# Rotated queries and keys of the second layer through SBUF with their low parts on GpSimd, and the norm after the out projection done in PSUM

## The chip, the core and the metric

The program runs on one core of one Trainium2 chip. The metric is the device time of one execution in microseconds (us). TensorE (PE, with its weight loads PEld), VectorE (DVE), ScalarE (ACT) and GpSimd (POOL) work side by side, each through its own instructions in the order in which the program has them; nearly all DMAs are issued by SyncE (SP), in order too. An instruction that waits therefore holds up all that stands behind it on its engine.

## The reference, cut to what matters

One inference step of a trunk of two layers over a prompt of 1024 tokens and 8 single sample tokens that attend to 2048 cached ones. Layer 0 has forgetting attention (12 heads of 64), layer 1 differential attention with rotary positions (6 heads of 2 x 64). Both have four more heads on a memory, one joint out projection, and a SwiGLU.

```python
# layer 1
q = rope(z[..., :w].reshape(b, t, 2 * N_HEADS_DIFF, HEAD_DIM), pos)
k = rope(z[..., w:2 * w].reshape(b, t, 2 * N_HEADS_DIFF, HEAD_DIM), pos)
s1 = einsum('bqhd,bkhd->bhqk', qb[..., :HEAD_DIM], k[..., :HEAD_DIM]) * HEAD_DIM ** -0.5   # s2 likewise
weights = masked_softmax(s1, mask) - lam * masked_softmax(s2, mask)
...
# both layers
h = h + rms_norm(merged @ w_out, g_post_mix)
u = rms_norm(h, g_pre_ffn) @ w_gate_up
```

## The kernel before

All is fp32. A matmul operand is split into a high part (a copy that TensorE's fast fp32 form rounds, `hi`, on ACT) and a low part (source minus high part, `lo`), and a projection is three products: high x high, high x low, low x high. The prompt's tokens, with the samples at their end, lie in three thirds of 384, 384 and 264 columns.

In `mixer` a loop goes over six pairs of heads, `hp`. While the attention of pair `hp` runs (`parts`, as steps that `beat` places between matmuls), `project` makes the queries (a = 0), keys (1) and values (2) of pair `hp + 1`, each for three thirds: nine blocks of 24 matmuls (`mm3`). A block adds up in one bank of PSUM with the tag "g". There are two such banks, so a block cannot begin until the last reader of the block two before it is done. In layer 1 a block of queries or keys goes on like this:

- `rope`: DVE shuffles neighbouring rows out of the bank into `sw` in SBUF (L998), POOL multiplies `sw` by the sine table (L999), DVE multiplies the bank by the cosine table in place (L1001) and adds `sw` to it in place (L1002).
- queries, `q_split`: ACT scales each half (64 rows) by 0.125 from the bank into `qq` (L403), SP copies it to the other half's place (L404), DVE makes the low part `ql` from the bank (L406).
- keys, `k_split`: ACT copies the bank to `f` (L1175), from which the outputs are transposed later (`natural`), then makes the high parts `kk` (L170); DVE makes the low parts (L173, `kk<-g,kk`).

Then come the scores `s_d` (two matmuls a piece, with `qq` and `ql`), `peaks` on DVE (L447: adds the causal rows, negates and takes the peak), the exponential on ACT (L463), the merge of the two weightings on DVE (`p_d`, L552), transposes `tp_d`, and the product with the values `av_d`. ACT moves that into `ao_d` (L1191), DVE norms it later (L1199), SP stores it (L1201). The memory heads have `ao_m` with the same tag "ao" (L519, L520).

Alongside runs `decode`: SP loads a page of cached keys `kp` (L602), POOL multiplies it by the query (L616), DVE adds up (L620), and the buffer is free for another page.

After the mixer, `finish_tile` with a name that begins with "o" handles a tile of 128 tokens after the out projection (8 tiles and the samples in each layer, in the groups FA, FB, FC of three): TensorE transposes the tile into `y_o`, two banks with the tag "s2" of which there is one set; ACT squares and adds up (L338), ACT copies `y_o` to `yn_o` in SBUF (L170); DVE and POOL make the root (L329, L333); DVE multiplies (L387) and adds to `h_o` (L388). A second norm of the sum (L338, L345) gives what TensorE transposes back (`xt_o`) for the FFN.

TensorE's order is pinned to the order in which the program was written; for the other engines a list scheduler sets it when the program is built.

Of the kernel before, what the change touches and what calls it, by code (L numbers as in the profile page):

```python
# [9 lines left out]
F32 = mybir.dt.float32  # L10
# [3 lines left out]
ALU = mybir.AluOpType  # L14
# [81 lines left out]
class Step:  # L96
# [274 lines left out]
    def finish_tile(self, pool, acc, o, ti, hsrc, hdst, g_post, g_pre, x, name, wait, row=None):  # L371

        nc = self.nc
        r = self.rows(ti)
        h = self.load_h(pool, ti, hsrc, f"h_{name}")
        y = pool.tile([128, D], F32, name=f"yn_{name}", tag="nat")
        if row is None:
            yp = self.b2(f"y_{name}")
            for k in range(8):
                self.pe.transpose(yp[:r, k * 128 : (k + 1) * 128], acc(k)[:, o : o + r], self.ident)  # L380
            ss = self.sumsq(pool, yp[:r], r, y, f"sy_{name}")
            self.hi(y[:r], yp[:r])
            row = y
        else:
            ss = self.sumsq(pool, row[:r], r, y, f"sy_{name}")
        rs = self.rstd(pool, ss[:r], r, D, f"ry_{name}")
        nc.vector.scalar_tensor_tensor(y[:r], row[:r], rs[:r], g_post[:r], op0=ALU.mult, op1=ALU.mult)  # L387
        nc.vector.tensor_tensor(h[:r], h[:r], y[:r], op=ALU.add)  # L388
        nc.sync.dma_start(hdst(ti), h[:r])
        if x is not None:  # L390
            self.norm(pool, h, r, g_pre, y, name)
            yield wait
            self.to_x(y, r, lambda tv, k0: [(tv, x[:, k0 : k0 + 4])], o, name)


    def q_split(self, src, n, c0, qq, ql):


        nc = self.nc
        part = lambda a, e, c: a[64 * e : 64 * e + 64, c : c + n]  # L400
        for e in range(2):
            same = part(qq[e], e, c0)
            nc.scalar.activation(same, part(src, e, 0), AF.Copy, scale=0.125)  # L403
            nc.sync.dma_start(part(qq[e], 1 - e, c0).bitcast(F32), same.bitcast(F32))  # L404
        for e in range(2):
            nc.vector.scalar_tensor_tensor(  # L406
                part(ql[e], e, c0), part(src, e, 0), 0.125, part(qq[e], e, c0).bitcast(F32),
                op0=ALU.mult, op1=ALU.subtract,
            )

    def k_split(self, src, n, c0, kk):
# [4 lines left out]
        for e in range(2):  # L416
            self.lo(part(kk[e], 1 - e, c0), part(src, e, 0), part(kk[e], e, c0))
# [22 lines left out]
    def peaks(self, pool, s, last, bias, name):  # L440
# [3 lines left out]
        if last is not None:  # L444
# [3 lines left out]
            out=s, in0=s, in1=bias, scale=-1.0, scalar=3e38, op0=ALU.add, op1=ALU.min, accum_out=nm  # L448
# [77 lines left out]
    def self_part(self, pool, qq, ql, kk, vs, subs, qb, bias, width, done, name):  # L526
# [9 lines left out]
        def make(i, e):  # L536
            b = bias(e, w)
            s, last = self.scores(qq[e], ql[e], kk[e], qb, w, f"s_{name}{e}")
            nm = self.peaks(pool, s, last if merge is None else None, b, f"{name}{e}")
# [453 lines left out]
    def rope(self, pool, ps, n, t, st, name):  # L993

        nc = self.nc
        sw = pool.tile([128, 384], F32, name=f"rs_{name}", tag="rsw")
# [5 lines left out]
        nc.vector.tensor_tensor(ps[:, :n], ps[:, :n], sw[:, :n], op=ALU.add)  # L1002
# [38 lines left out]
    def mixer(self, l, xs, st, begin):  # L1041
# [5 lines left out]
        with ExitStack() as cx:  # L1047
# [3 lines left out]
            if l == 1:  # L1051
# [3 lines left out]
                {**bufs, **{f"ql{i}{e}": 1 for i in range(2) for e in range(2)}, "kvf": 6 - 3 * l, "pt": 3 - l, "ao": 7 - 2 * l, "at": 1, "sm": 16, "st": 8},  # L1055
# [95 lines left out]
            def project(hp, r, units=(0, 1, 2), thirds=(0, 1, 2)):  # L1151
                for a in units:
# [8 lines left out]
                    for t in thirds:  # L1161
# [7 lines left out]
                        if a < 2 and l == 1:  # L1169
                            self.rope(main, ps, n, t, st, nm)  # L1170
                        if a == 0:
                            self.q_split(ps, n, t0 * 128, r["qq"], r["ql"])
                        else:
                            f = main.tile([128, 384], F32, name=f"f{nm}", tag="kvf")
                            nc.scalar.activation(f[:, :n], ps[:, :n], AF.Copy)  # L1175
                            if a == 1:
                                self.k_split(ps, ks(t), t0 * 128, r["kk"])
                            self.spawn(natural(a, t, hp, f, r), RD if a == 1 and l == 1 else 4.0)
# [531 lines left out]
```

## Time and profile before

| | us |
|---|---|
| median of 3 runs | 3060.92 |
| lowest and highest | 3060.40, 3066.18 |
| the profiled execution | 3070.34 |
| its span, first to last instruction | 3068.5 |
| PE busy in the span | 2806.3 |
| DVE, ACT, POOL busy | 2068.0, 1767.4, 1107.1 |

The profile is of one execution, whose own time is 9.4 us above the median. Busy times of different engines overlap. For TensorE the profile also gives the granted clock, as a share of 2.4 GHz; its two levels here are 1.00 and 0.50. Layer 1's mixer stands at 1557 to about 2140 us of the span; its six projections of queries, keys and values end at about 2006 us. The norms after the out projection stand at 630 to 735 (layer 0) and 2155 to 2260 us (layer 1), and the short third of each near 1300 and 2810 us.

### The profile page before, as it was taken

To read this page: it belongs to the slowest core of one execution; us is meant where nothing else is said; L and a number is where in the kernel's file an instruction comes from. 1 tells how busy PE (TensorE), PEld (TensorE's weight loads), DVE (VectorE), ACT (ScalarE), POOL (GpSimd) and SP (SyncE) were. 2 spreads that over 40 slices of the span, in tenths; PEclk is the share of its full clock that TensorE was granted. 3 is DMA by queue.
4 is the path that set the end of the run, shared out by engine and by line. 5 is a ranking of instruction groups with operands and counts; after the bars stand their busy time and mean duration, and the time that the engine had idled before them with its cause. 6 is when DMAs were issued, how large, how long until landed. Compare 5 with 4: busy or idle time off the path is not lost. (4 is left out here: it accounts for less than half of the span.)

```text
span 3068.5 us, 53791 instructions
## 1 busy us (share of the span) xinstructions
PE 2806.3 (91%) x17567; PEld 2647.2 (86%) x17567; DVE 2068.0 (67%) x3645; ACT 1767.4 (58%) x4617; POOL 1107.1 (36%) x840
## 2 busy tenths in 40 slices
PE   7999998878999999999988888888888999999998
PEld 5899998877888998999977878888877899899998
DVE  7566666577678777386466778755887667654655
ACT  6445555444678886355554554465543689864544
POOL 3345556422211111244434556564232111113443
PEclk9999999989999999999999999899998999999999
DMA  5555566486556654356645444464775566644764
GB/s 167 154 154 162 161 170 184 115 263 201 165 184 198 200 191 160 109 164 196 185 148 154 125 124 123 125 179 144 249 229 172 176 226 220 204 148 128 226 180 132
DMA packets 523979, 529.01 MB, mean 172 GB/s; under 512 B 54957, under 2 KB 416078, under 8 KB 523698
## 3 DMA queue, kind: packets, MB, share of 16 engines
q1 hardware_dynamic: 523554, 524.79, 56.2%
q8 instruction: 138, 2.26, 0.3%
q14 instruction: 143, 1.17, 0.1%
q0 software_dynamic: 144, 0.79, 0.1%
HBM read 477.82 MB, written 39.24 MB: 169 GB/s over the span
## 5 line engine op out<-in xcount | busy, mean ns | idle before, releaser
L700 ACT ACTIVATE vp<-vp,s 128x64 f32<-128x64 f32 (+1 forms) x1680 | 462.5, 358 | 119.0 <-DMA vp<-in_cache_fox_v_dram 67.7
L81 PE MATMUL ga<-xf,h_g 128*128 128x384 f32 (+1 forms) x2112 | 499.3, 324 | 0.0
L81 PE MATMUL gu<-xf,h_u 128*128 128x384 f32 (+1 forms) x2112 | 495.1, 321 | 0.0
L81 PE MATMUL g<-xi,h_w 128*128 128x384 f32 (+2 forms) x1728 | 438.7, 340 | 49.7 <-DVE kk L173 23.8
L616 POOL TENSOR_TENSOR kp<-kp,qb 128x768 f32<-128x768 f32 x186 | 344.1, 1852 | 324.5 <-DMA kp<-in_cache_fox_k_dram 140.8
L81 PE MATMUL dn<-h_d,gt 128*128 128x512 f32 x1056 | 352.9, 408 | 20.1 <-ACT gt L170 16.4
L81 PEld LDWEIGHTS ga<-xf,h_g 128*128 128x128 f32 x2112 | 368.2, 191 | 2.0 <-ACT fa L1434 0.2
L81 PEld LDWEIGHTS gu<-xf,h_u 128*128 128x128 f32 x2112 | 365.0, 189 | 0.2
L81 PEld LDWEIGHTS g<-xi,h_w 128*128 128x128 f32 x1728 | 304.5, 197 | 60.8 <-DVE ql L406 26.0
L81 PE MATMUL ga<-xf,l_g 128*128 128x384 f32 (+1 forms) x1056 | 339.4, 321 | 0.0
L81 PE MATMUL gu<-xf,l_u 128*128 128x384 f32 (+1 forms) x1056 | 338.6, 321 | 0.8 <-POOL l_u L173 0.8
L173 POOL TENSOR_TENSOR l_u<-r_u,h_u 128x512 fp32r<-128x512 f32 x96 | 135.1, 1407 | 496.1 <-ACT h_u L170 489.3
L708 DVE TENSOR_TENSOR acc<-acc,vp 128x768 f32<-128x768 f32 x240 | 248.9, 1043 | 77.3 <-ACT vp L700 75.9
L81 PE MATMUL g<-xi,l_w 128*128 128x384 f32 (+2 forms) x864 | 284.9, 330 | 3.8 <-DVE rs_x L329 1.9
L173 POOL TENSOR_TENSOR l_d<-r_d,h_d 128x512 fp32r<-128x512 f32 x96 | 136.1, 1418 | 401.9 <-ACT h_d L170 370.0
L1436 DVE TENSOR_TENSOR fa<-fa,dn 128x512 f32<-128x512 f32 (+1 forms) x400 | 227.5, 578 | 65.3 <-PE dn L81 64.2
L81 PEld LDWEIGHTS dn<-h_d,gt 128*128 128x128 f32 x1056 | 203.7, 194 | 75.9 <-ACT gt L170 20.5
L81 PE MATMUL dn<-l_d,gt 128*128 128x512 f32 x528 | 214.2, 406 | 9.1 <-DVE l_d L173 8.2
L173 POOL TENSOR_TENSOR l_g<-r_g,h_g 128x512 fp32r<-128x512 f32 x96 | 140.6, 1465 | 200.2 <-ACT h_g L170 197.9
L170 ACT ACTIVATE h_u<-r_u 128x512 fp32r<-128x512 f32 x192 | 120.0, 628 | 149.0 <-PE dn L81 59.2
L81 PEld LDWEIGHTS ga<-xf,l_g 128*128 128x128 f32 x1056 | 200.8, 190 | 0.0
L81 PEld LDWEIGHTS gu<-xf,l_u 128*128 128x128 f32 x1056 | 199.1, 189 | 1.1 <-POOL l_u L173 1.0
(590 smaller groups left out, 6305.8 us busy)
## 6 DMA issues: line engine op xcount, KB each, us to landing
kp<-in_cache_fox_k_dram SPq DMA_DIRECT2D x128, 384.0 KB
r_g<-in_w_gate_up_dram SPq DMA_DIRECT2D x192, 256.0 KB
r_u<-in_w_gate_up_dram SPq DMA_DIRECT2D x192, 256.0 KB
r_d<-in_w_down_dram SPq DMA_DIRECT2D x192, 256.0 KB
vp<-in_cache_fox_v_dram SPq DMA_DIRECT2D x128, 384.0 KB
kp<-in_cache_diff_k_dram SPq DMA_DIRECT2D x128, 384.0 KB
vp<-in_cache_diff_v_dram SPq DMA_DIRECT2D x128, 384.0 KB
r_wo<-in_w_out_dram SPq DMA_DIRECT2D x96, 256.0 KB
```

What stands on the lines that cost most here:

```text
L81: self.pin(self.eng.matmul(out, w, x, **k), max(n, 256) if x.dtype == F32R else 2 * max(2 * n, 256))
L170: self.nc.scalar.activation(out, src, AF.Copy)
L173: (eng or self.nc.vector).tensor_tensor(out, src, hi.bitcast(F32), op=ALU.subtract)
L616: r = eng.tensor_tensor(k, k, q, op=ALU.mult)
L700: nc.scalar.activation(dst[:, hs], v[:, hs], AF.Copy, scale=wv[:, b, h, g : g + 1])
L708: todo.append(nc.vector.tensor_tensor(acc[b], acc[b], v, op=ALU.add))
L1436: self.last_v = nc.vector.tensor_tensor(dst, dst, o, op=ALU.add).ins.name
```

## The change

It has three parts.

1. In layer 1 `rope`'s last addition writes a new tile `f` in SBUF (tag "kvf") instead of the bank; `q_split` and `k_split` read `f`, so that the addition is the bank's last reader. ACT's copy of the keys to `f` goes. The low parts are made by POOL. The queries are no longer scaled by 0.125; `peaks` applies the factor to the scores.
2. The buffers of layer 1's mixer: "kvf" has 4 instead of 3, "ao" 3 instead of 5.
3. In `finish_tile`, where the name begins with "o", ACT's copy of `y_o` goes; DVE multiplies in place in PSUM and adds from there, so that the addition is the last reader of `y_o`.

```diff
@@ finish_tile
-        y = pool.tile([128, D], F32, name=f"yn_{name}", tag="nat")
+        y = at = pool.tile([128, D], F32, name=f"yn_{name}", tag="nat")
...
-            self.hi(y[:r], yp[:r])
-            row = y
+            if name[0] == "o":
+
+                row = at = yp
+            else:
+                self.hi(y[:r], yp[:r])
+                row = y
...
-        nc.vector.scalar_tensor_tensor(y[:r], row[:r], rs[:r], g_post[:r], op0=ALU.mult, op1=ALU.mult)
-        nc.vector.tensor_tensor(h[:r], h[:r], y[:r], op=ALU.add)
+        nc.vector.scalar_tensor_tensor(at[:r], row[:r], rs[:r], g_post[:r], op0=ALU.mult, op1=ALU.mult)
+        nc.vector.tensor_tensor(h[:r], h[:r], at[:r], op=ALU.add)
@@ q_split (its scale is a new argument, 0.125 by default), k_split (eng, None by default)
-            nc.scalar.activation(same, part(src, e, 0), AF.Copy, scale=0.125)
+            nc.scalar.activation(same, part(src, e, 0), AF.Copy, scale=scale)
...
+            if scale == 1.0:
+                self.lo(part(ql[e], e, c0), part(src, e, 0), part(qq[e], e, c0), nc.gpsimd)
+                continue
...
-            self.lo(part(kk[e], 1 - e, c0), part(src, e, 0), part(kk[e], e, c0))
+            self.lo(part(kk[e], 1 - e, c0), part(src, e, 0), part(kk[e], e, c0), eng)
@@ peaks (scale is 0.125 where the two weightings are merged, layer 1)
-            out=s, in0=s, in1=bias, scale=-1.0, scalar=3e38, op0=ALU.add, op1=ALU.min, accum_out=nm
+            out=s, in0=s, in1=bias, scale=-scale, scalar=3e38, op0=ALU.add, op1=ALU.min, accum_out=nm
@@ rope
+        f = pool.tile([128, 384], F32, name=f"rf_{name}", tag="kvf")
...
-        nc.vector.tensor_tensor(ps[:, :n], ps[:, :n], sw[:, :n], op=ALU.add)
+        nc.vector.tensor_tensor(f[:, :n], ps[:, :n], sw[:, :n], op=ALU.add)
+        return f
@@ mixer
-"kvf": 6 - 3 * l, "pt": 3 - l, "ao": 7 - 2 * l,
+"kvf": 6 - 2 * l, "pt": 3 - l, "ao": 7 - 4 * l,
@@ project
                         if a < 2 and l == 1:
-                            self.rope(main, ps, n, t, st, nm)
-                        if a == 0:
+                            f = self.rope(main, ps, n, t, st, nm)
+                            if a == 0:
+                                self.q_split(f, n, t0 * 128, r["qq"], r["ql"], 1.0)
+                            else:
+                                self.k_split(f, ks(t), t0 * 128, r["kk"], nc.gpsimd)
+                        elif a == 0:
```

TensorE's own order does not change. On POOL, where the queries of the fourth pair of heads are made, the program before has these rows (`rs<-rs,tab` is the sine multiplication of a third, 384, 384 and 256 wide; `kp` a page; `l_w` a low part of weights):

```order
L999 TENSOR_TENSOR rs_23314<-rs_23314,tab_20410 128x384
L616 TENSOR_TENSOR kp_10_1_23389<-kp_10_1_23389,qb_1_22668 128x768
L616 TENSOR_TENSOR kp_11_1_23465<-kp_11_1_23465,qb_1_22668 128x768
L999 TENSOR_TENSOR rs_23433<-rs_23433,tab_20411 128x384
L616 TENSOR_TENSOR kp_12_1_23557<-kp_12_1_23557,qb_1_22668 128x768
L173 TENSOR_TENSOR l_w_23548<-r_w_23544,h_w_23546 128x8x2x32
L173 TENSOR_TENSOR l_w_23872<-r_w_23868,h_w_23870 128x512
L999 TENSOR_TENSOR rs_23518<-rs_23518,tab_20411 128x256
```

and the changed one, at the same place:

```order
L1010 TENSOR_TENSOR rs_23306<-rs_23306,tab_20402 128x384
L626 TENSOR_TENSOR kp_10_1_23381<-kp_10_1_23381,qb_1_22662 128x768
L173 TENSOR_TENSOR ql_20376<-rf_23305,qq_23230 64x384
L173 TENSOR_TENSOR ql_20377<-rf_23305,qq_23231 64x384
L626 TENSOR_TENSOR kp_11_1_23458<-kp_11_1_23458,qb_1_22662 128x768
L1010 TENSOR_TENSOR rs_23426<-rs_23426,tab_20402 128x384
L626 TENSOR_TENSOR kp_12_1_23551<-kp_12_1_23551,qb_1_22662 128x768
L173 TENSOR_TENSOR l_w_23542<-r_w_23538,h_w_23540 128x8x2x32
L173 TENSOR_TENSOR ql_20376<-rf_23425,qq_23230 64x384
L173 TENSOR_TENSOR ql_20377<-rf_23425,qq_23231 64x384
L173 TENSOR_TENSOR l_w_23863<-r_w_23859,h_w_23861 128x512
L1010 TENSOR_TENSOR rs_23512<-rs_23512,tab_20402 128x256
```

Two low parts of a third now stand ahead of the next third's sine multiplication.

On DVE, from the second third's addition to the third third's cosine, before:

```order
L1002 TENSOR_TENSOR g_23344<-g_23344,rs_23433 128x384
L447 ISA s_d_23498,nm_d_23501<-s_d_23498,zm 128x384
L447 ISA nm_d_23501 128x1
L620 TENSOR_REDUCE s_20345<-kp_11_1_23465 128x12
L552 SCALAR_TENSOR_TENSOR p_d_23401<-p_d_23449,f_d_23477,p_d_23401 128x256
L998 STREAM_SHUFFLE rs_23518<-g_23458 128x256
L1001 TENSOR_TENSOR g_23458<-g_23458,tab_20410 128x256
L406 SCALAR_TENSOR_TENSOR ql_20385<-g_23344,qq_23239 64x384
L406 SCALAR_TENSOR_TENSOR ql_20386<-g_23344,qq_23240 64x384
```

and in the change:

```order
L1013 TENSOR_TENSOR rf_23425<-g_23336,rs_23426 128x384
L561 TENSOR_SCALAR f_d_23470<-r_d_23221,l_d_23220,le 128x1
L454 ISA s_d_23491,nm_d_23494<-s_d_23491,zm 128x384
L454 ISA nm_d_23494 128x1
L630 TENSOR_REDUCE s_20336<-kp_11_1_23458 128x12
L562 SCALAR_TENSOR_TENSOR p_d_23393<-p_d_23442,f_d_23470,p_d_23393 128x256
L1009 STREAM_SHUFFLE rs_23512<-g_23451 128x256
L1012 TENSOR_TENSOR g_23451<-g_23451,tab_20401 128x256
```

The bank `g` has its last reader at the first row instead of the last one.

On ACT, in the norms after layer 0's out projection, around the second norm's sum of tile 1 (`yn_o,ss_o<-h_o`) and the first of tile 2 (`yn_o,sy_o<-y_o`), before:

```order
L338 ACTIVATE yn_o_8822,ss_o_8843<-h_o_8820 128x1024
L170 ACTIVATE h_g_9213<-r_g_9211 128x512
L1364 ACTIVATE yo_8642<-wo_9027 128x384
L338 ACTIVATE yn_o_8955,sy_o_8965<-y_o_8956 128x1024
L170 ACTIVATE yn_o_8955<-y_o_8956 128x1024
L170 ACTIVATE xf_8639<-xt_o_9066 128x4x128
```

and in the change:

```order
L338 ACTIVATE yn_o_8821,ss_o_8841<-h_o_8819 128x1024
L338 ACTIVATE yn_o_8953,sy_o_8963<-y_o_8954 128x1024
L170 ACTIVATE h_wo_9134<-r_wo_9132 128x512
L170 ACTIVATE h_wo_9140<-r_wo_9138 128x512
L1381 ACTIVATE yo_8642<-wo_8930 128x384
```

The copy of `y_o` is gone, and tile 2's first sum has moved up, ahead of `yo_8642` for which it stood behind before.

## Rows read from the trace of the kernel before

**Rows 1.** Windows: sum, busy us of PE, PEld, DVE, ACT, POOL; PEclk, DMA, GB/s.
```profile
1557.00:1640.00 83.00, 63.82 (x422) 56.56 (x421) 50.03 (x99) 46.18 (x92) 26.25 (x27) 0.92 0.52 163
1640.00:2006.00 366.00, 311.06 (x1916) 295.65 (x1915) 285.52 (x622) 181.88 (x484) 210.26 (x162) 0.92 0.44 127
630.00:735.00 105.00, 82.85 (x469) 80.17 (x468) 90.03 (x111) 52.84 (x92) 29.42 (x28) 0.90 0.73 233
```

**Rows 2.** PE's waits, 1550 to 2006 us: total us, times, longest us.
```profile
PE g L81 <- DVE kk L173: 23.8, 11, 5.2
PE g L81 <- DVE ql L406: 23.8, 6, 8.5
PE tp_d L84 <- DVE p_d L552: 12.2, 5, 2.8
```

**Rows 3.** Timeline, one wait on queries: start us, us; [idle before <-releaser].
```profile
1807.83 1.84 POOL L616 TENSOR_TENSOR kp<-kp,qb 128x768 f32<-128x768 f32 x1 [8.20 <-DMA kp<-in_cache_diff_k_dram]
...
1809.63 1.72 POOL L999 TENSOR_TENSOR rs<-rs,tab 128x384 f32<-128x384 f32 x1
...
1811.38 0.56 DVE L1002 TENSOR_TENSOR g<-g,rs 128x384 f32<-128x384 f32 x1 [0.71 <-POOL rs L999]
...
1815.26 1.11 DVE L406 SCALAR_TENSOR_TENSOR ql<-g,qq 64x384 fp32r<-64x384 f32 x2
...
1816.42 1.01 PE L81 MATMUL g<-xi,h_w 128*128 128x384 f32 x2 [4.15 <-DVE ql L406]
```

**Rows 4.** Timeline around one wait on keys.
```profile
1762.05 0.56 DVE L1002 TENSOR_TENSOR g<-g,rs 128x384 f32<-128x384 f32 x1
...
1768.14 0.98 PE L81 MATMUL g<-xi,h_w 128*128 128x384 f32 x2 [3.48 <-DVE kk L173]
```

**Rows 5.** Timeline: the first addition of layer 1 and the wait behind it.
```profile
1568.13 0.54 DVE L1002 TENSOR_TENSOR g<-g,rs 128x384 f32<-128x384 f32 x1
...
1571.01 1.01 PE L81 MATMUL g<-xi,h_w 128*128 128x384 f32 x2 [8.47 <-DVE ql L406]
```

**Rows 6.** Busy time by stretch, right behind that wait on keys.
```profile
1768.10:1771.00 2.90, 2.86 (x9) 2.89 (x10) 2.81 (x7) 0.85 (x3) 2.90 (x4) 0.50 0.39 138
1771.00:1775.00 4.00, 4.00 (x29) 3.97 (x28) 3.70 (x5) 1.09 (x3) 1.37 (x2) 0.98 0.63 179
```

**Rows 7.** Groups by line and form: count, busy us, mean ns, idle before.
```profile
L173 DVE TENSOR_TENSOR kk<-g,kk 64x384 fp32r<-64x384 f32 x48 | 26.6, 555 | 5.7 <-ACT kk L170 5.0
L999 POOL TENSOR_TENSOR rs<-rs,tab 128x384 f32<-128x384 f32 x24 | 25.7, 1069 | 34.6 <-DVE rs L998 27.2 <-DMA tab<-in_c_rope_dram 7.4
```

**Rows 8.** Groups by line and form: the merge on DVE.
```profile
L552 DVE SCALAR_TENSOR_TENSOR p_d<-p_d,f_d,p_d 128x640 f32<-128x640 f32 x6 | 12.3, 2048 | 0.0
L552 DVE SCALAR_TENSOR_TENSOR p_d<-p_d,f_d,p_d 128x1024 f32<-128x1024 f32 x6 | 8.3, 1392 | 0.0
```

**Rows 9.** POOL's waits, 1640 to 2006 us.
```profile
POOL kp L616 <- DMA kp<-in_cache_diff_k_dram: 103.5, 40, 8.2
```

**Rows 10.** Timeline of the norms after layer 0's out projection.
```profile
654.27 1.91 PE L84 MATMUL y_o<-cm,yo 128*128 128x128 f32 x8
...
658.89 2.06 DVE L388 TENSOR_TENSOR h_o<-h_o,yn_o 128x1024 f32<-128x1024 f32 x1
...
684.58 1.94 PE L84 MATMUL xt_o<-cm,yn_o 128*128 128x128 f32 x8 [8.94 <-DVE yn_o L345]
```

**Rows 11.** Groups by line and form: copy, sum, DVE in PSUM.
```profile
L170 ACT ACTIVATE yn_o<-y_o 128x1024 f32<-128x1024 f32 x16 | 16.4, 1024 | 0.3
L388 DVE TENSOR_TENSOR h_o<-h_o,yn_o 128x1024 f32<-128x1024 f32 x16 | 22.6, 1414 | 0.0
L447 DVE CUSTOM_DVE_ANT_1 s_d<-s_d,zm 128x1024 f32<-128x1024 f32 x12 | 14.7, 1223 | 3.9 <-PE s_d L81 3.9
```

**Rows 12.** Timeline of the memory heads of layer 1.
```profile
2040.93 0.76 ACT L519 ACTIVATE ao_m<-av_m,rl_m 128x64 f32<-128x64 f32 x2 [0.74 <-PE av_m L81]
...
2043.05 0.32 SPq L1201 DMA_DIRECT2D mN<-ao_d  x1
```

More of the change, by code (lines that the diff above doesn't have):

```diff
@@ L393, in finish_tile, with q_split @@
             self.to_x(y, r, lambda tv, k0: [(tv, x[:, k0 : k0 + 4])], o, name)
-    def q_split(self, src, n, c0, qq, ql):
+    def q_split(self, src, n, c0, qq, ql, scale=0.125):
         nc = self.nc
@@ L409, in q_split, with k_split @@
             )
-    def k_split(self, src, n, c0, kk):
+    def k_split(self, src, n, c0, kk, eng=None):
         part = lambda a, e, c: a[64 * e : 64 * e + 64, c : c + n]
@@ L438, in two, with peaks @@
         return ap[:, :w] if w <= 512 else ap[:, :w].rearrange("p (a b) -> p a b", a=2)
-    def peaks(self, pool, s, last, bias, name):
+    def peaks(self, pool, s, last, bias, name, scale=1.0):
         nc = self.nc
@@ L538, in make @@
             s, last = self.scores(qq[e], ql[e], kk[e], qb, w, f"s_{name}{e}")
-            nm = self.peaks(pool, s, last if merge is None else None, b, f"{name}{e}")
+            nm = self.peaks(
+                pool, s, last if merge is None else None, b, f"{name}{e}", 1.0 if merge is None else 0.125
+            )
             yield
@@ L1054, in mixer @@
                 cx.enter_context(tc.tile_pool(name=f"at{l}", bufs=1, reuse_waits="tile")),
-                {**bufs, **{f"ql{i}{e}": 1 for i in range(2) for e in range(2)}, "kvf": 6 - 3 * l, "pt": 3 - l, "ao": 7 - 2 * l, "at": 1, "sm": 16, "st": 8},
+                {**bufs, **{f"ql{i}{e}": 1 for i in range(2) for e in range(2)}, "kvf": 6 - 2 * l, "pt": 3 - l, "ao": 7 - 4 * l, "at": 1, "sm": 16, "st": 8},
                 {"rsw": "kvf", "nt": "kvf"},
@@ L1177, in project @@
                                 self.k_split(ps, ks(t), t0 * 128, r["kk"])
+                        if a:
                             self.spawn(natural(a, t, hp, f, r), RD if a == 1 and l == 1 else 4.0)
```

## The prediction

> **What bounds the kernel now.** I read the busy times by stretch first, then the waits of TensorE in the stretch that the change touches, then the timeline around single waits. While the five later pairs of heads are projected, TensorE is busy for 311.1 of 366 us (85%), VectorE for 285.5 (78%), ScalarE for 181.9 (50%) and GpSimd for 210.3 (57%) [rows 1]. So TensorE is the bound, with 54.9 us of idle time there and 19.2 in the 83 us ahead, where the first pair is projected. The waits say what ends most of this idle time: a block of a projection that cannot begin because its bank "g" is still read, 11 times by a key's low part (23.8 us) and 6 times by a query's (23.8 us), 47.6 us in all; waits for the merge come behind with 12.2 [rows 2].
>
> One wait shows the chain. The addition of rope ends at 1811.38 + 0.56 = 1811.94; TensorE began to wait at 1816.42 - 4.15 = 1812.27, and waits through VectorE's other work and the two low parts (1815.26, 1.11 us) [rows 3]. With the bank free at the addition, TensorE would have been 0.33 us from waiting at all. On the keys it is the same with more room: the addition ends at 1762.61, the wait begins at 1768.14 - 3.48 = 1764.66, 2.05 us later [rows 4].
>
> **The mixer: the wait.** The addition now is the bank's last reader, so what a wait loses is all that lay behind the addition's end. In the two above that is the whole wait. The longest, 8.47 us, began at 1571.01 - 8.47 = 1562.54, and its addition ended only at 1568.67, so 6.1 of it stay [rows 5]. 47.6 - 6.1 = 41.5 us can go.
>
> **The mixer: the clock.** Behind a wait TensorE runs slowly for a while. After the wait on keys the granted clock is 0.50 (the lower of its levels, 1.2 GHz) for 2.9 us, with 9 matmuls done, and 0.98 in the next 4.0 us, with 29 [rows 6]. At the second pace 2.9 us hold 21, so such a stretch costs 2.9 x (1 - 9/21) = 1.7 us at the most; with gaps in the records I take 1.3. For some 12 of the 17 waits, which are long enough, that is 16 us. TensorE by itself could thus give 41.5 + 16 = 57 us, about 48 of them in the five later pairs.
>
> **The mixer: VectorE.** It can't follow TensorE all the way. It loses 48 low parts of 384 columns at 0.555 us [rows 7] and 24 of 256, for which I estimate 0.555 x 256/384 = 0.37: 35.5 us, five sixths of it (29.6) in the five pairs. It gains waits for GpSimd. The merge with 640 columns takes 2.05 us on average, the one with 1024 only 1.39 [rows 8]: something other than columns costs 0.66 us and more. If that is GpSimd's work on SBUF at the same time, it grows with GpSimd's share. This rises from 57% to about 81% (below); some 80 merges and norms of `ao_d` with two operands in SBUF lie in these 366 us, so 80 x 0.24 x 0.66 = 13 us. VectorE then has 285.5 - 29.6 + 13 = 269 us. At its share of today (78%) they need 345 us, a gain of 21; at 85%, which I take for the most that order and heads' changes leave, 316, which is TensorE's own limit of 48 or so. The middle is 35, and the first pair, with less work beside it, gives 7 of its 9: **42 us** for the mixer, bounds 0 (other waits take over) and 57.
>
> **The mixer: GpSimd.** No row shows a low part of 64 x 384 there. The sine multiplication, also with two operands of 384 columns, takes 1.07 us [rows 7]; a page's 768 columns take 1.84 [rows 3], so 0.92 for 384; the slowest sine shown took 1.72 [rows 3]. Rows don't seem to count: on VectorE 64 x 384 takes 0.555 [rows 7], 128 x 384 0.56 [rows 4]. I take 1.07, bounds 0.92 and 1.72: 48 x 1.07 + 24 x 0.71 = 68 us (59 to 110), 57 of it in the five pairs. GpSimd then has 267 of some 330 us, 81%. What covers it is that it waits there 103.5 us, 40 times, for pages to land [rows 9]. If that cover is gone, what stands behind the low parts is late: the next sine multiplication, the addition, and with it the bank. The first score that reads a low part comes after the three blocks of values, so the low parts themselves are not urgent.
>
> **What costs nothing.** The factor 0.125 goes into an operation of VectorE that has a scale already. ScalarE reads `f` in SBUF where it read the bank, and loses 18 copies; at 50% it waits for others, so neither shows. The queries' `f` needs a buffer that they did not have, and one is added to three; a reader that holds one long would stop the addition, at the price of the waits that are there now. SP issues the same copies of `qq` after the same two ScalarE operations.
>
> **The three "ao" buffers.** In layer 1's memory heads `ao_m` would take, with three, a buffer whose `ao_d` is stored from 2043.05 on, while ScalarE is ready at 2040.93 [rows 12]: 2043.37 - 2040.93 = 2.4 us at least. Two later ones look alike, 7 us on ScalarE with `av_m` and TensorE behind it. I take **+4**, bounds 0 and 10, since a store's landing is not in the row.
>
> **The norms after the out projection.** 18 copies of 1.02 us go from ScalarE, and VectorE's sum, at 1.414 us from SBUF [rows 11], should take the 1.22 of an operation in place in PSUM: 3.5 us less for 18. VectorE is the bound there, 90.0 of 105 us, TensorE has 22 idle and ScalarE is busy half the time [rows 1]. Half of the copies, 9 us, and the 3.5 make 12 at best. Against it, `y_o` is held until the addition and has one set of banks: tile 2's transposes ran at 654.27, while the addition of tile 1 ended at 658.89 + 2.06 = 660.95, so they come 6.7 us later [rows 10]. Read in this way the pairs of tiles in both layers come to 29 us, of which this is the longest. But TensorE stops soon after anyway, up to 8.94 us, for VectorE's result [rows 10], and VectorE takes the tiles one after the other whatever `y_o` does. I take **-6**, bounds -12 and +29.
>
> The sum: -42 - 6 + 4 = -44 us. The profiled execution takes 3070.3 us (3068.5 of span); it becomes 3026. It stands 9.4 above the median of 3060.9, which becomes **3017**.
>
> **The rivals.**
> 1. *TensorE alone bounds* (VectorE follows): all 57 and the whole 12 with little on "ao", some -65: 2996. For it speaks that VectorE is idle 22% today; against it that right behind a wait it is nearly always busy, 2.81 of 2.90 and 3.70 of 4.00 us [rows 6].
> 2. *GpSimd and VectorE lock each other out.* If all 80 two-operand instructions pay 0.66 us more, it is 53 us, VectorE has 285.5 - 29.6 + 53 = 309, and at 85% that is 363: 3 us gained in the five pairs, perhaps 4 in the first: -7 - 6 + 4 = -9, 3052. For it speaks the price of the merge [rows 8] and the sine of 1.72 [rows 3]; against it that a GpSimd that is busy 57% should already show most of this. The Trainium skill (SBUF — State Buffer, section "SBUF: two separate sides") calls the port pair of the two engines an exclusive lock, in which an instruction with two operands in SBUF fully blocks while the other engine's runs. By that rule every low part moved takes time from VectorE's remaining work; the two merge rows agree with it, and no row tells how often it strikes after the move.
> 3. *The held `y_o` is not absorbed*: +29 in place of -6: 3052.
> 4. *Slower: GpSimd is late.* If 2 us of low parts stand ahead of each third's sine multiplication and find no gap, the addition comes later by them and by the page that comes first. It decides where the delay exceeds the room and the wait that is gone, on the keys 2.05 + 3.48 = 5.5 us [rows 4]. One page that lands 8.2 late and is multiplied (1.84) [rows 3] with two low parts (2.1) is 12 us. If that hits a dozen of the 30 blocks of queries and keys at about 5.5 + 0.8 each, the 42 become -9, and with +4 and -6 the sum is +7: 3068.
> 5. *The bank's waits come back as others* at the same places, for merges or pages: 0 for the mixer, 3057 to 3061.
>
> **How the numbers follow.** Chances: the forecast 0.48 (own range 3000 to 3032), rivals one to five 0.14, 0.13, 0.10, 0.09, 0.06. A change of 0.2% (6 us) is about what a measurement of this kernel can tell from none. The forecast, the first rival and most of the second and third are faster: 0.80; the last, and parts of the second to fourth, the same: 0.11; most of the fourth slower: 0.09. To leave out no more than 0.2 the range goes from 2994, just below the first, to 3055, above the second and third.
>
> **What would show it.** In the profile after, "g" waits should name the addition or a shuffle, total under 12 us in 1550 to 2006 with the first (6.1) among them; the layer's last projection should end some 40 us earlier; the low parts should read near 1.07 us on GpSimd, whose share rises to some 80%; VectorE's merges should grow by some tenths. In the norms, TensorE's new waits for `y_o` should be matched by shorter ones for `xt_o`. I'd be wrong if additions wait for the sine multiplication by more than 3 us often, if merges take over 2.5 us, if ScalarE's wait for an "ao" buffer holds the memory heads, or if the norms' stretch gets longer.

## The result, and the profile after

The change takes 3027.6 us (median of 4 runs, 3018.9 to 3033.1) where the kernel before takes 3063.6 beside it, with a ratio of 0.9878 (95% interval 0.9849 to 0.9907), 36 us less by the medians. In a second set of runs (below) it was 0.9896 (0.9877 to 0.9914), 31 us less by the medians. Forecast were 3017 us and 44 less, with a range of 2994 to 3055. The sign and the place were as forecast. One step of the mechanism failed, that the additions of `rope` stay where they were, and the term of the mixer was too large for it.

Stretches are compared between the same matmuls here, because everything behind a change moves. "First pair" goes from the first matmul on a bank "g" of layer 1 to the first score of layer 1, "five pairs" from there to the end of the last matmul on "g", "memory heads" from there to the first transpose into `y_o` of layer 1, "norms" from layer 0's first transpose into `y_o` to the matmul `smt_d`, some 50 us behind these norms in the program. All in us, from one profile each; the ratio is that of the timed runs to those of the kernel before in the same set.

| kernel | ratio (95%) | first pair | five pairs | memory heads | norms |
|---|---|---|---|---|---|
| before | 1 | 96.7 | 362.5 | 147.4 | 149.4 |
| before, second profile | | 97.8 | 360.1 | 145.8 | 149.1 |
| the change | 0.9878 (0.9849, 0.9907) | 95.4 | 332.8 | 153.6 | 143.7 |
| e5: the change again | 0.9896 (0.9877, 0.9914) | 95.3 | 334.3 | 150.8 | 143.1 |
| e1: mixer only | 0.9944 (0.9920, 0.9967) | 93.7 | 337.9 | 150.2 | 148.4 |
| e2: norms only | 0.9977 (0.9957, 0.9997) | 99.0 | 357.5 | 145.6 | 139.1 |
| e3: low parts on VectorE | 0.9954 (0.9936, 0.9972) | 93.3 | 356.2 | 149.7 | 141.1 |
| e4: sine on VectorE | 0.9939 (0.9910, 0.9967) | 94.2 | 348.9 | 152.2 | 140.9 |
| e6: low parts behind sine | 0.9895 (0.9877, 0.9913) | 98.7 | 333.1 | 155.9 | 141.0 |
| e7: ao_m elsewhere | 0.9909 (0.9888, 0.9930) | 95.3 | 337.8 | 147.5 | 142.8 |
| e8: low parts twice | 1.0008 (0.9992, 1.0024) | 99.1 | 360.6 | 151.8 | 139.2 |
| e9: weights' low parts split | 0.9948 (0.9930, 0.9965) | 94.3 | 347.8 | 150.5 | 143.6 |
| e10: head norm off VectorE | 0.9856 (0.9843, 0.9870) | 94.2 | 324.2 | 153.1 | 143.2 |
| e12: e10 with ao_m elsewhere | 0.9850 (0.9824, 0.9876) | 93.8 | 325.0 | 148.6 | 139.7 |

Where the same code is profiled twice, a stretch moves by 2 to 5 us (332.8, 334.3 and 337.8 or 337.9 for five pairs that are alike; 357.5 to 362.5 for the old ones); smaller differences say nothing.

The five pairs by the windows of the profile, which answer to [rows 1]: first the kernel before in its second profile, then the change. Columns: the stretch, its sum, busy us of PE, PEld, DVE, ACT, POOL, then PEclk, DMA share and GB/s.

```profile
1642.86:2002.94 360.08, 308.27 (x1933) 295.71 (x1933) 283.93 (x616) 180.38 (x483) 209.96 (x167) 0.93 0.44 128
```

```profile
1638.51:1971.32 332.81, 296.93 (x1933) 283.22 (x1933) 272.04 (x558) 178.72 (x469) 273.11 (x226) 0.97 0.46 137
```

TensorE has the same matmuls and is busy 11 us less, at a granted clock of 0.97 after 0.93, and it is idle 36 us after 52. VectorE loses 12 us, GpSimd gains 63. Idle time gives 16 us of the 27, the clock 11. GpSimd found its room in the waits for pages, which answer to [rows 9] (1610 to 1960 us of the change):

```profile
POOL kp L626 <- DMA kp<-in_cache_diff_k_dram: 28.1, 17, 4.0
```

TensorE's waits of the change in both stretches of projections, which answer to [rows 2] (total us, times, longest):

```profile
PE g L81 <- DVE rf L1013: 29.1, 14, 6.2
PE tp_d L84 <- DVE p_d L562: 9.3, 5, 2.5
```

The low parts no longer end a wait, as forecast. But 14 waits for the bank are still there, 29.1 us of them where under 12 were forecast, and all of them end with the addition. This is what the experiments had to explain.

One of these waits in the timeline of the change (start us, us, engine); the rows are the third third of the keys:

```profile
1679.18 2.36 DVE L562 SCALAR_TENSOR_TENSOR p_d<-p_d,f_d,p_d 128x1024 f32<-128x1024 f32 x1
1680.42 2.26 POOL L173 TENSOR_TENSOR l_w<-r_w,h_w 128x512 fp32r<-128x512 f32 x1
...
1681.48 0.45 DVE L1009 STREAM_SHUFFLE rs<-g 128x264 f32<-128x264 f32 x1
...
1683.15 1.84 POOL L626 TENSOR_TENSOR kp<-kp,qb 128x768 f32<-128x768 f32 x1
...
1683.33 1.81 DVE L1216 SCALAR_TENSOR_TENSOR ao_d<-ao_d,rs_d005p,gsub 128x128 f32<-128x128 f32 x1
...
1684.93 1.36 POOL L173 TENSOR_TENSOR l_w<-r_w,h_w 128x512 fp32r<-128x512 f32 x1
...
1685.07 1.77 DVE L562 SCALAR_TENSOR_TENSOR p_d<-p_d,f_d,p_d 128x512 f32<-128x512 f32 x1
1686.25 1.19 POOL L1010 TENSOR_TENSOR rs<-rs,tab 128x264 f32<-128x264 f32 x1
1686.76 0.94 DVE L630 TENSOR_REDUCE s<-kp 128x12 f32<-128x768 f32 x1
...
1687.62 0.42 DVE L1013 TENSOR_TENSOR rf<-g,rs 128x264 f32<-128x264 f32 x1
...
1688.10 1.01 PE L81 MATMUL g<-xi,h_w 128*128 128x384 f32 x2 [2.77 <-DVE rf L1013]
```

Two things are to be seen. The shuffle is done at 1681.93, but the sine multiplication that needs it starts only at 1686.25: GpSimd has a page and two low parts of weights before it, without a gap worth naming. And two of VectorE's instructions with two operands in SBUF end only behind GpSimd's: the norm of `ao_d` at 1685.14, when the page is done at 1684.99, the merge at 1686.84, when the weights' low part is done at 1686.29. Each of the five pairs has this wait in the same place, at 2.7 to 2.8 us, and one of 1.0 to 1.6 on the second third, where two new low parts (`kk`) stand right ahead of the sine multiplication.

The same holds on the mean. Over the 30 blocks of queries and keys in the five pairs the sine multiplication starts 2.5 us behind the end of its shuffle (2.6 in e5), where it was 0.8 and 0.9 in the two profiles before, and the addition ends 5.2 us behind the start of the shuffle, where it was 3.9 and 4.0. So the additions come 1.2 us later than they did.

### The profile page after: what moved, and what is told of

Read it like the earlier page. It is cut to its first block, busy times and chain, and to the rows that moved or that the text cites. A ratio compares the mean times of both kernels' runs of the same rounds, so it can differ in the third digit from the quotient of the medians.

```text
span 3031.4 us, 53767 instructions
## 1 busy us (share of the span) xinstructions
PE 2793.3 (92%) x17567; PEld 2636.9 (87%) x17567; DVE 2054.9 (68%) x3573; ACT 1746.5 (58%) x4581; POOL 1180.0 (39%) x912
## 3 DMA queue, kind: packets, MB, share of 16 engines
q8 instruction: 138, 2.26, 0.3%
## 4 chain that ended last, share of the span: by engine, by line
PE 62%; DVE 14%; DMA 10%; ACT 5%; issue 5%; POOL 3%; SPq 1%; ACTq 0%; DVEq 0%; POOLq 0%
PE dn L81 14%; PE ga L81 13%; PE gu L81 11%; PE g L81 7%; PE wo L81 4%; ACT vp L710 2%; PE av_f L81 2%; DMA kp<-in_cache_diff_k_dram 2%; DMA vp<-in_cache_fox_v_dram 2%; DVE kp L626 2%; PE s_f L81 1%; DMA kp<-in_cache_fox_k_dram 1%; PE tp_f L84 1%; PE s_d L81 1%; DVE s L630 1%
## 5 line engine op out<-in xcount | busy, mean ns | idle before, releaser
L81 PE MATMUL g<-xi,h_w 128*128 128x384 f32 (+2 forms) x1728 | 434.6, 337 | 30.7 <-DVE rf L1013 29.1
```

Source lines behind the costliest of these rows:

```text
L81: self.pin(self.eng.matmul(out, w, x, **k), max(n, 256) if x.dtype == F32R else 2 * max(2 * n, 256))
```

## The experiments

**e1 and e2: the parts alone.** e1 takes the third part back, e2 puts it alone into the kernel before.

```diff
-            if name[0] == "o":
-                row = at = yp
-            else:
-                self.hi(y[:r], yp[:r])
-                row = y
+            self.hi(y[:r], yp[:r])
+            row = y
```

> The changed kernel with the norm after the out projection as before (ScalarE's copy back, y_o free after it). Theory A (the parts add up; the profile after puts -31 us on the five later pairs' projections, +5 on the memory heads, some -8 on the norms): 0.990 of before, 7 to 9 us above the whole change. Rival (the norms' part gives nothing, what it saves comes back as waits for y_o): 0.988, as the whole change. Rival (the held y_o costs): 0.986 or less.

> The kernel before with only the norm after the out projection done in PSUM. Theory A: 0.997 (-8 us, between -5 and -11), TensorE's waits for xt_o fall by more than 20 us and 20 to 27 us of new waits for y_o stand against them. Rival (given back): 0.999 to 1.001. Rival (the held y_o costs): 1.002 or more.

Measured were 0.9944 and 0.9977, 17 and 7 us less by the ratios, together 24 with some 9 of uncertainty; the change's ratios give 37 and 32. The parts add up within that; that they help one another is neither shown nor excluded. The norms' part by itself gives 1 to 13 us. TensorE's waits in the whole program show where it does not come from. The kernel before (second profile), then the change:

```profile
PE xt_o L84 <- DVE ry_o L329: 17.7, 6, 4.9
PE xt_o L84 <- DVE yn_o L345: 17.4, 4, 6.7
...
PE xt_o L84 <- DVE mt L173: 1.4, 1, 1.4
```

```profile
PE y_o L84 <- DVE h_o L392: 26.4, 6, 6.6
...
PE xt_o L84 <- DVE yn_o L345: 4.5, 2, 4.0
...
PE xt_o L84 <- DVE mt L173: 4.0, 3, 2.0
...
PE xt_o L84 <- DVE ry_o L329: 1.8, 2, 1.4
```

26.4 us of new waits for `y_o` come, and 26.2 of the waits for `xt_o` go (36.5 before, 10.3 after): TensorE waits in another place for the same engine, and gains nothing by that. The gain stands behind the norms. In layer 0's stretch of the table (632.90 to 782.30 us before, 638.96 to 782.70 in the change) TensorE's other waits for VectorE are, before and then in the change:

```profile
PE dn L81 <- DVE l_d L173: 5.5, 1, 5.5
PE smt_d L84 <- DVE r_d L846: 5.0, 1, 5.0
```

```profile
PE dn L81 <- DVE l_d L173: 3.7, 1, 3.7
```

The wait for `r_d` is 4.9 to 5.4 us in the three profiles without this part and gone in all with it; the one for `l_d` is 5.5 to 7.2 us without it and 0.3 to 3.7 with it. VectorE is busy 116.1 us in this stretch after 120.4, and its sum (the addition to `h_o`) takes 1.21 us after 1.41. This fits a VectorE that is done with the norms sooner. The stretch is 139 to 144 us in all kernels with this part, and 148 to 149 in those without it.

**e3: low parts on VectorE.** The bank is released as in the change, GpSimd gets nothing new.

```diff
-                self.lo(part(ql[e], e, c0), part(src, e, 0), part(qq[e], e, c0), nc.gpsimd)
+                self.lo(part(ql[e], e, c0), part(src, e, 0), part(qq[e], e, c0))
...
-                                self.k_split(f, ks(t), t0 * 128, r["kk"], nc.gpsimd)
+                                self.k_split(f, ks(t), t0 * 128, r["kk"])
```

> The changed kernel, but VectorE makes the low parts of queries and keys, from f in SBUF: the bank is still released at the addition, GpSimd gets no new work, VectorE loses none. Theory P (what is left of the bank's waits comes from GpSimd's sine multiplications standing behind the new low parts): waits for the addition fall from 29 to 15 us or less, time equal to the changed kernel or up to 8 us less (0.985 to 0.988). Rival V (VectorE's queue holds the addition, so its load decides): waits for the addition rise to 35 or more, time 0.992 to 0.996.

```profile
1629.12:1985.31 356.19, 300.48 (x1933) 284.46 (x1933) 302.20 (x619) 180.59 (x469) 218.95 (x166) 0.97 0.44 128
```

```profile
PE s_d L81 <- ACT p_d L470: 28.4, 17, 4.0
PE g L81 <- DVE rf L1013: 23.9, 8, 6.6
```

```profile
L173 DVE TENSOR_TENSOR kk<-rf,kk 64x384 fp32r<-64x384 f32 x24 | 33.0, 1374 | 0.8
L173 DVE TENSOR_TENSOR ql<-rf,qq 64x384 fp32r<-64x384 f32 x24 | 20.2, 841 | 0.4
```

The five pairs take 356 us. With the bank released but the low parts left on VectorE some 5 of the 28 us are gained, no more than a stretch moves by itself, and the move of the low parts gives the other 22 to 23 (ratio 0.9954, as rival V had it). This is not the price of the release alone, because e3 changes one thing more: VectorE's low parts now read both operands from SBUF, and take 1.37 and 0.84 us where they took 0.55 from the bank [rows 7]. The 60 of the five pairs take 58 us on VectorE here, as long as on GpSimd in the change (59); from the bank they took 30. Neither theory had the waits right: those for the bank go down a little, to 23.9, and waits for a bank of scores come (5.4 in the change in this stretch and the one before it, 28.4 here). VectorE is busy 302 of 356 us and is now itself what comes late: the sine multiplication starts 0.9 us behind its shuffle, as before the change, and the addition still ends 5.2 us behind the shuffle's start.

**e4: sine on VectorE.** `nc.gpsimd.tensor_tensor(sw, ...)` in `rope` becomes `nc.vector.tensor_tensor`, so the addition waits for nothing of GpSimd.

> The changed kernel with rope's sine multiplication on VectorE, so that the addition waits for nothing of GpSimd; VectorE gets 36 instructions, some 20 us, GpSimd loses 31. Theory P: the waits for the addition fall from 29 to under 12 us (the first one, 6, stays), time 8 to 15 us below the changed kernel (0.983 to 0.986). Rival V: they stay at 25 or more, time as the changed kernel or up to 15 us more (0.988 to 0.993).

```profile
1641.76:1990.63 348.87, 302.51 (x1933) 289.55 (x1933) 290.47 (x588) 179.33 (x467) 245.66 (x196) 0.95 0.46 131
```

```profile
PE g L81 <- DVE rf L1013: 21.1, 12, 5.6
PE tp_d L84 <- DVE p_d L562: 16.5, 5, 4.0
PE s_d L81 <- ACT p_d L470: 14.9, 9, 5.6
```

The bank's waits fall only to 21.1, between the two theories; others grow, the stretch is 15 us longer than in e5, and the time (0.9939) is where rival V had it, or a little above. Taking GpSimd out of the chain doesn't pay if VectorE has to do the work.

**e5: the change again**, and **e6: low parts behind the sine.** In e6 the low parts of a third are kept until the next third's `rope` and ordered behind its sine multiplication.

```diff
                             f = self.rope(main, ps, n, t, st, nm)
+                            flush(self.sine)
...
+            def flush(behind=None):
+                for low in self.lates:
+                    ins = low()
+                    if behind:
+                        self.order(ins, behind)
+                self.lates.clear()
```

> The change itself again, so that the variants below stand beside it in one set of runs. Theory A (the parts add up): the mixer's 18 us of the run with the mixer alone and the norms' 6 make 0.992. Rival (the two help one another, or the first set was a lucky one or the last an unlucky one): 0.988 as at first.

> The change, with each third's low parts made behind the next third's sine multiplication on GpSimd (an order between two of its instructions, nothing else). Theory P (the low parts hold the sine multiplication): the waits for the addition fall from 28 to 29 us to 22 or less (the ones of 1.0 us on the second third of the keys go), time 4 to 8 us below the change. Rival W (pages and low parts of weights ahead of the third third's sine hold it, the waits of 2.8 us): waits 24 to 28 us, time within 3 us of the change. Rival F (the buffers of f are held longer and the additions wait for one): slower than the change by 5 us or more.

e5 gave 0.9896; its interval (0.9877 to 0.9914) holds the rival's 0.988 and ends just short of theory A's 0.992, which has an uncertainty of its own. e6 gave 0.9895 and the same 333 us in the five pairs:

```profile
1637.23:1970.34 333.11, 295.52 (x1933) 281.37 (x1933) 260.55 (x556) 178.70 (x467) 271.14 (x225) 0.97 0.49 137
```

```profile
PE g L81 <- DVE rf L1017: 26.3, 13, 6.2
```

Time and sum of the waits are as rival W had them (e5 has 29.5), but the waits themselves have moved. Those on the second third of the keys are gone, as theory P said, and on the last third they are 1.0 to 1.6 us in four of the five pairs (2.5 in the other) where the change has 2.7 to 2.9. In their place waits of 1.2 to 2.9 us come on the first third of the keys, where pages now stand ahead of the sine multiplication:

```profile
1730.46 2.56 POOL L630 TENSOR_TENSOR kp<-kp,qb 128x768 f32<-128x768 f32 x1
...
1731.26 0.59 DVE L1013 STREAM_SHUFFLE rs<-g 128x384 f32<-128x384 f32 x1
...
1733.49 1.84 POOL L630 TENSOR_TENSOR kp<-kp,qb 128x768 f32<-128x768 f32 x1
...
1735.29 1.35 POOL L1014 TENSOR_TENSOR rs<-rs,tab 128x384 f32<-128x384 f32 x1
...
1738.28 0.54 DVE L1017 TENSOR_TENSOR rf<-g,rs 128x384 f32<-128x384 f32 x1
...
1738.88 0.51 PE L81 MATMUL g<-xi,h_w 128*128 128x264 f32 x2 [2.23 <-DVE rf L1017]
```

So the low parts do hold the sine multiplication that they stand ahead of, but taking them away moves the wait to another block. VectorE is busy 261 us here, 11 to 15 less than in the two profiles of the change, and the stretch is no shorter.

**e7: ao_m elsewhere.** `ao_m` of layer 1 takes a buffer with the tag "kvf" in place of "ao".

> The change, with the memory heads' ao_m in layer 1 in the buffers with the tag kvf, which the projections no longer use by then, so that nothing there waits for the three ao buffers. Theory A (the three buffers cost the 4 to 6 us that the memory heads' stretch grew by): 3 to 6 us below the change. Rival (the stretch is set by something else): within 2 us of it.

The time can't be told from that of e5 (0.9909 and 0.9896, each with 0.002). The stretch of the memory heads can: 147.5 and, in e12, 148.6 us, where the nine profiles with three "ao" buffers for both have 149.7 to 155.9. With five buffers it is 145.6 to 147.4. So the three buffers cost some 4 us of this stretch, which no difference in the whole time shows. ScalarE waits 3.5 and 6.0 us there for stores of `ao_m` in the change and in e5, and not at all before. In e7 such waits are still there, four of 4.4 us together.

**e8: low parts twice.** Each `self.lo` on GpSimd is issued twice, with the same output.

> The change, with every low part made twice by GpSimd (the second writes the same values), 68 us more for it, 57 of them in the five later pairs: 277 us of 350 become 334. Theory P (GpSimd's queue holds the sine multiplications): the waits for the addition grow from 29 to 50 us or more, time 15 to 35 us above the change. Rival S (there is room in GpSimd's waits for pages): waits up by 8 at most, time up by 0 to 5 us. The price of a clash: if merges and norms of ao_d with two operands in SBUF get longer with GpSimd's share, the mean of the merges grows by 0.1 to 0.3 us.

```profile
1635.27:1995.90 360.63, 301.37 (x1933) 285.17 (x1933) 277.80 (x560) 180.37 (x470) 325.79 (x284) 0.95 0.44 127
```

```profile
PE g L81 <- DVE rf L1015: 42.8, 14, 5.6
PE g L81 <- DVE rs_d L329: 11.1, 5, 2.2
```

GpSimd is busy 326 of 361 us (90%), TensorE waits 54 us for the bank, and the whole gain is gone: 1.0008. Of 52 us of GpSimd's work, 26 come out at the end of the five pairs. So at the change's 82% half of this further work is paid for in time, and theory P holds in this direction: the sine multiplication now starts 4.0 us behind its shuffle and the addition ends 6.6 us behind the shuffle's start (2.6 and 5.2 in e5). The merges' mean does not grow (1.36 us after 1.35 and 1.40); that of the norms of `ao_d` does, from 1.06 and 1.11 to 1.21.

**e9: weights' low parts split.** `wp.even = True` becomes `wp.even = l == 0`.

> The change, with every second low part of layer 1's weights in the five later pairs on VectorE instead of GpSimd (16 of 32: 24 us less for GpSimd, 13.6 more for VectorE). The stretch of these pairs in the runs so far goes by both engines' busy time: 52 us more for GpSimd made it 26 us longer (0.5 a us; low parts twice), 28 more for VectorE with 54 less for GpSimd made it 22 longer, so 1.7 a us for VectorE. Theory B (both engines' load counts, at these prices): +24 - 12 = 12 us longer than with the change, 0.993. Theory P (what stands ahead of the sine multiplication on GpSimd is what is left): the waits for the addition fall to 22 us or less, 5 to 10 us below the change, 0.987.

```profile
1635.64:1983.48 347.84, 299.05 (x1933) 285.51 (x1933) 278.59 (x577) 179.52 (x469) 256.65 (x211) 0.95 0.47 133
```

```profile
1679.16 2.00 DVE L173 TENSOR_TENSOR l_w<-r_w,h_w 128x512 fp32r<-128x512 f32 x1
...
1681.09 2.02 DVE L562 SCALAR_TENSOR_TENSOR p_d<-p_d,f_d,p_d 128x1024 f32<-128x1024 f32 x1
...
1683.04 0.45 DVE L1009 STREAM_SHUFFLE rs<-g 128x264 f32<-128x264 f32 x1
...
1689.28 1.01 PE L81 MATMUL g<-xi,h_w 128*128 128x384 f32 x2 [5.02 <-DVE rf L1013]
```

The waits for the addition grow to 38.9 us, so theory P is out. The five pairs are 13.5 us longer than in e5, as theory B said (12), but not for its reason: VectorE's busy time grows by 2.9 us and not 13.6, GpSimd's falls by 17, and at 1.7 and 0.5 a us that would be 4 us less. The rows show the place: VectorE's low part of the weights takes 2.0 us, and the shuffle of the third third comes behind it and a merge; four of the five pairs wait 4.8 to 5.0 us there, where in the change all five wait 2.7 to 2.8. A price for each engine's busy time did not forecast this edit; what stands ahead of the shuffle was what moved.

**e10: head norm off VectorE.** The timeline above points at instructions in which VectorE waits for GpSimd. The norm of `ao_d` is the worst of them for its size; it waits in 28 of its 48 instances in the change and takes 1.3 us or more in 26, in the kernel before in 16.

```diff
-                            r = nc.vector.scalar_tensor_tensor(o, o, rs, st["gsub"], op0=ALU.mult, op1=ALU.mult)
-                            self.order(r, self.last_v)
+                            nc.scalar.activation(o, o, AF.Copy, scale=rs)
+                            nc.gpsimd.tensor_tensor(o, o, st["gsub"], op=ALU.mult)
```

> The change, with the norm of ao_d in two steps, ScalarE's scale and GpSimd's product with gsub, instead of one of VectorE, which waits for GpSimd in most of its 48 instances (0.35 us where it does not, 1.4 to 2.1 where it does). VectorE loses some 55 us of busy time in the five pairs, GpSimd gets 40 instructions of 128x128, some 18 us. Theory B: at 1.7 and 0.5 us a us far more than TensorE can give, so TensorE bounds: the stretch falls from 333 to 310 or 320, time 15 to 25 us below the change, 0.981 to 0.985. Rival L (the time is the shared port's and moves on to the merges): merges grow by 0.3 us or more, 0 to 5 us below the change. Rival O (the three ao buffers are held longer and ScalarE waits for them): slower than the change.

```profile
1637.46:1961.61 324.15, 293.17 (x1933) 277.94 (x1933) 226.99 (x522) 192.23 (x504) 285.08 (x261) 0.98 0.49 140
```

```profile
L1217 POOL TENSOR_TENSOR ao_d<-ao_d,gsub 128x128 f32<-128x128 f32 x48 | 25.7, 538 | 3.6 <-ACT ao_d L1216 1.8 <-DMA kp<-in_cache_diff_k_dram 0.8 <-PE wo L81 0.5
```

VectorE is busy 227 us instead of 276, GpSimd 285 instead of 274, the stretch is 10 us shorter, and the kernel is at 0.9856 (0.9843 to 0.9870): theory B's direction, but less than it said (310 to 320 us for the stretch, 0.985 at most). Rival L is out: the mean of the merges over their eight widths, 1.35 and 1.40 us in the two profiles of the change, is 1.31. But 49 us off VectorE gave 10. Of the 44 us that the norms took in e5, 13 are their own (38 of 0.35) and the rest is waiting; which of the two the 10 us are owed to, e10 does not tell. At 70% it is no longer what is late; 26.8 us of waits for the bank are still there, and GpSimd is at 88%.

**e11: a second look at before.**

> The kernel before, for a second profile of it: how far its stretches move between two executions, beside which the differences above are to be read. Theory A: the five pairs' stretch within 5 us of 362.5, the bank's waits within 3 us of 47.6. Rival (that profile was an outlier): outside of these.

Theory A for the stretch (360.1 and 362.5). The bank's waits are 30.1 and 21.1 us, 51.2 in all, against 47.6, a little outside.

**e12: both.**

> The version that the runs point to: the change with the norm of ao_d on ScalarE and GpSimd (as in the run with the head norm off VectorE) and ao_m in the kvf buffers. Theory A (the two add up): 0.983 to 0.985, 0 to 5 us below the run with the head norm alone (0.9856), and the memory heads' stretch shorter by 3 us or more. Rival (with the norm gone from VectorE the three buffers no longer hold anything): as that run, 0.985 to 0.987, the stretch the same.

0.9850 (0.9824 to 0.9876): the best of the kernels run, 43 us below before by the medians (3018.6 and 3061.2), though it can't be told from e10. The memory heads are 4.5 us shorter than in e10, the five pairs the same, as theory A had it.

## Why the prediction was right, and where it was too large

**Right: what bounds, and what goes.** The bank's release and the move together shorten the projections, and the low parts end no wait any more. What the release gives by itself is not shown (e3), and neither the fourth "kvf" buffer nor the copies that ScalarE loses were run alone. **The clock** came out right: TensorE's busy time in the five pairs falls by 11 to 14 us against 13, five sixths of the 16 forecast. This is in part luck. By the records of the granted clock TensorE spent 55 and 51 us of the five pairs at 0.50 in the two profiles before, and not the 29 of ten stretches of 2.9 us that the forecast reckoned with, and it still spends 20 there: the forecast had the stretches too small and took all of them to go. The 2.77 us wait shown above still costs clock (the two us behind it; columns as above):

```profile
1688.10:1690.10 2.00, 2.00 (x6) 2.00 (x7) 0.00 (x0) 1.30 (x3) 1.84 (x3) 0.50 0.62 156
```

**GpSimd** was right: low parts of 1.14 and 1.07 us where 1.07 was taken from the sine multiplication [rows 7], a share of 82% (81% forecast):

```profile
L173 POOL TENSOR_TENSOR ql<-rf,qq 64x384 fp32r<-64x384 f32 x24 | 27.5, 1144 | 2.1 <-ACT qq L407 1.2
L173 POOL TENSOR_TENSOR kk<-rf,kk 64x384 fp32r<-64x384 f32 x24 | 25.7, 1069 | 3.4 <-ACT kk L170 1.8
```

**VectorE's sum** was near: 272 and 276 us (e5) against 269. The low parts took 30 us off it, as forecast; the waiting for GpSimd in merges and norms added 15 to 20 where 13 was put. Its share of the stretch is 82%, in the middle of the 78 and 85% from which the term was taken. The prediction had no reason for the middle, so that it was met is luck.

**Too large: the mixer's 42 us.** The five pairs gave 22 to 30 instead of 35 and the first pair 2 instead of 7. So the term measured 24 to 32 us. The step that failed is behind the 41.5 us of waits that "can go": 18 to 22 went. It read, from two waits, that with the bank free at the addition all that lay behind the addition is gained, and took the additions to stay where they were. They came 1.2 us later on the mean, 5.2 us behind the shuffle's start after 3.9 and 4.0. e8 shows that GpSimd's load moves them (6.6 us), e3 and e9 that what stands on VectorE does. I had costed this as a rival that decides from 5.5 us of delay, all or nothing; what happened is a part of it in every one of the five pairs, 1.0 to 1.6 us on the second third of the keys and 2.7 to 2.8 on the third. One of the signs of being wrong that the prediction gave, additions that wait for the sine multiplication by more than 3 us often, came in part: on the last third of the queries and on the keys that multiplication starts 3.2 to 4.3 us behind its shuffle, where it was 0.1 to 1.5 before (means of the five pairs).

**The rival of the shared port** was out as priced: the merges' mean over eight widths grew from 1.22 to 1.35 and 1.40 us, that of the norms of `ao_d` from 0.81 and 0.87 to 1.06 and 1.11, 0.1 to 0.3 each and not 0.66. Together these instructions took 79 and 81 us of the five pairs before and 96 and 99 in the change, 15 to 20 more and not 53. Which width is struck changes: of the two in [rows 8] the wider is now the slow one.

```profile
L562 DVE SCALAR_TENSOR_TENSOR p_d<-p_d,f_d,p_d 128x1024 f32<-128x1024 f32 x6 | 13.2, 2194 | 0.0
...
L562 DVE SCALAR_TENSOR_TENSOR p_d<-p_d,f_d,p_d 128x640 f32<-128x640 f32 x6 | 8.7, 1454 | 0.0
```

But the rival was not empty. In the rows above VectorE's instructions end behind GpSimd's, and e10, which takes 40 of them from VectorE in the five pairs, gives 10 us, though with their own time as well as their waiting. The Trainium skill (SBUF — State Buffer, section "SBUF: two separate sides") says that an instruction of VectorE with two operands in SBUF and one of GpSimd that reads SBUF exclude each other: the one that starts first holds the shared port pair for its whole length. The rows agree: a norm of `ao_d` takes 1.81 us there, and 0.35 where nothing is in its way, as here in the trace of the kernel before:

```profile
2033.34 0.35 DVE L1199 SCALAR_TENSOR_TENSOR ao_d<-ao_d,rs_d502p,gsub 128x128 f32<-128x128 f32 x1 [0.66 <-POOL rs_d502p L333]
```

What does not hold is my price, which grew with GpSimd's share: with the low parts twice the merges' mean is 1.36 us, no more than in the change, and in e6, at a share of 81%, it is 1.21, as before the change. Nor does this waiting alone set the time, since e6 has less of it and no shorter stretch.

**The low parts' new place** was right though it could have gone the other way. The Trainium skill (Perfetto Trace Analysis, section "Optimizing Scalar/DVE Operations") warns that moving work between these two engines might not help, because of that port. Here it does: 22 us of the five pairs for 55 us of GpSimd's time there (e3 beside e5), since that had waits for pages to put them in, and since VectorE needed as long for them once both operands lay in SBUF (58 us and 59).

**The three "ao" buffers** were right (+4; 3 to 6 in the memory heads' stretch), though the wait that shows is for a store of `ao_m` and not, as read in [rows 12], of `ao_d`. **The norms** were right too (-6; 7 by e2, with 1 to 13, and 5 to 10 in layer 0's stretch): the new waits for `y_o`, 26.4 us against the 29 read, are matched by 26.2 of those for `xt_o` that go, so the rival of the held `y_o` is out, and VectorE's sum takes 1.21 us where 1.22 was put. What layer 1's norms gave, 0 to 3 us, is within the noise of a profile.

**Open.** Whether the two parts help one another (24 us apart, 32 to 37 together, by the ratios); what the release of the bank gives by itself; and how much of the 27 us of waits that e10 leaves would go with an order on GpSimd that puts the sine multiplication ahead of pages and low parts of weights; e6 moved only the low parts of queries and keys.

## What to carry to other kernels

When a reader of a buffer is taken away, the wait falls to what the next to last reader allows, and that one must be followed back to what it waits for on its own engine and on the others, with the new work already in their queues. An engine that is idle 40% of the time has room for work only as far as its waits can be filled; the e8 kind of run, the same work twice, tells what the next microsecond of it costs. Instructions that take five times their own length beside another engine's can be found by comparing instances of one form; what moving them gives has to be run, for here 49 us off VectorE gave 10.

## What the runs showed of the hardware

VectorE's 128x128 norm with two operands in SBUF took 0.35 us alone. In the change 26 of its 48 instances took 1.3 to 1.9 us (16 in the kernel before), and each of them ended 0.15 us behind a page or a low part of weights on GpSimd. A low part of weights of 128x512 took 0.67 to 0.69 us on VectorE in eight instances of e9 and 1.84 to 2.01 in the other seven, which ended 0.55 us behind a page. Low parts of 64x384 took 0.55 us on VectorE from the bank and 0.84 and 1.37 on the mean with both operands in SBUF (e3). GpSimd, too, is held: its low part of 128x512 took 2.26 us beside a merge of 2.36 and 1.36 beside another. Doubling GpSimd's new work did not lengthen the merges further (1.36 us after 1.35 and 1.40), but the norms (1.21 after 1.06 and 1.11).
